# Five feed-forward sections with 13 Strassen groups in place of six with 11, and output chunks added in pairs

## Chip, core and metric

The kernel runs on one core of one Trainium2 chip. The metric is the device time of one execution in microseconds, as the median of several runs; beside it stands one execution under the hardware profiler.

## What is computed

Two residual blocks over 256 tokens of 2048 features, in float32, and a final norm. Each block is a mixer followed by a gated feed-forward part with 5632 hidden features:

```python
def swiglu(h, w_gate, w_up, w_down):
    return (jax.nn.silu(h @ w_gate) * (h @ w_up)) @ w_down

for i in range(DEPTH):            # 2
    h = h + mixer_i(h)            # conv and pooling, then a short conv
    h = h + swiglu(rms_norm(h, ffn_norm[i]), w_gate[i], w_up[i], w_down[i])
return rms_norm(h, final_norm)
```

## The kernel before

Features lie on the 128 partitions and tokens along the rows, so that a chunk is 128 features by 256 tokens; there are 16 chunks of the model width (`NC`) and 44 of the hidden width (`NF`). The residual `h` stays in SBUF throughout.

**A product in three matmuls.** To keep float32 accuracy, every operand is split in a rounded high half and the low rest. `halves_of` (L212) does it for weights: ScalarE copies the high half (L217), VectorE subtracts it to give the low half (L218). `product` (L309) multiplies one block of 128x128 weights with one chunk: high x high, high x low, low x high, three matmuls of 256 columns (L310 to L312), added up in one PSUM bank. A block is one such product.

**Weights** arrive in units of 16 blocks (1 MB) by DMAs from SP's queue (`fetch`, L206) into four buffers, in the order of use. `prepare` (L221) splits them in pieces: 8 blocks for plain units. Five buffers hold the high and five the low halves. `advance` (L250) runs before every block or step and prepares three pieces ahead (`LOOK`).

**The feed-forward part** (`swiglu`, L716) cuts the 44 hidden chunks in sections. `SECTIONS` (L55) lists (groups, direct chunks) of each: `SIZES` are then 9, 6, 8, 7, 7, 7. A *direct* chunk takes 2 x 16 blocks (gate and up, L816 to L840), then on VectorE two scalings by the norm (L476), a product with silu(gate) (L813) and the split into `y` (L336). A *group* makes two chunks at once with a Strassen scheme: in `s_stream` (L781) seven forms instead of eight products, tokens by 256 weight columns, 4 units of 14 steps, each step three matmuls (L794 to L796) into four PSUM banks `s`. A Strassen unit is prepared in four pieces, with the sums of weight blocks that the scheme needs on VectorE (L245 to L248). `combine` (L755) takes the forms together after the group's last unit, seven additions out of PSUM, two `silu` on ScalarE (L775) and two products (L776); `turned` (L745), 20 places later in the order, transposes the result with four TensorE transposes (L750) and splits it into `y` (L752, L753).

**Windows.** The parts of consecutive sections are interleaved. Window w of a feed-forward part holds section w's direct chunks and groups and the down-projection of section w-1: for each of the 16 output chunks one product for each of its hidden chunks, all in one bank out of the pool `acc` (three banks, which the direct chunks and transposes use too), then one addition to `h` (L848) on VectorE. There is one window more than sections, and in the last one the chunk goes on to the next norm (`following.add`, L850): in layer 0 ScalarE and VectorE split it for the second mixer (L338, L339), ScalarE squares it (L447) and GpSimd sums up (L449); in layer 1 ScalarE squares it and multiplies the gain in (L433), and after the 15th chunk it loads the table for the square root (L435). `merged` (L89) writes the order out: runs of 14 Strassen steps spread evenly among the window's plain blocks, after `LEAD` plain blocks (96 in window 0, where the norm and the operands of the Strassen forms are made ready) and before `TAIL` plain blocks (30 in the window of the last section). The two halves of `y` are used in turn by even and odd sections; their sizes follow from the largest section of each kind (`SLOT_A`, `SLOTS`, 9 + 7 slots of 2 KB per partition).

Everything outside `swiglu` is the first mixer (656 blocks), the second mixer (1024 blocks) and the closing norm (L904 to L915).

Of the kernel before, what the change touches and what calls it, by code (L numbers as in the profile page):

```python
# [14 lines left out]
ALU = mybir.AluOpType  # L15
PSUM = bass.MemoryType.PSUM

P = 128
T = 256
D = 2048  # L20
NC = D // P
# [30 lines left out]

SECTIONS = ((1, 7), (2, 2), (2, 4), (2, 3), (2, 3), (2, 3))  # L55
SIZES = [2 * g + p for g, p in SECTIONS]
FIRST = [sum(SIZES[:i]) for i in range(len(SIZES))]
SLOT_A = max(SIZES[0::2])
SLOTS = SLOT_A + max(SIZES[1::2])
LEAD = (96,) + (0,) * len(SECTIONS)  # L60
FORMS_AT, REST_AT = 28, 70
TAIL = (0,) * (len(SECTIONS) - 1) + (30, 0)

# [9 lines left out]
def section_order(i):  # L73

    g, p = SECTIONS[i]
    return list(range(2 * g, 2 * g + p)) + list(range(2 * g))


def window_counts(w):
    blocks = 0  # L80
    if w < len(SECTIONS):
        blocks += SECTIONS[w][1] * 2 * NC
    if w:
# [103 lines left out]
def block_kernel(ctx: ExitStack, tc: tile.TileContext, xT: bass.AP, xtok: bass.AP, vec: bass.AP, wall: bass.AP, out: bass.AP):  # L187
    nc = tc.nc
# [14 lines left out]
    def new_acc(shape=(P, T), name="acc"):  # L203
        return banks["acc"].tile(list(shape), F32, name=name, tag="acc")
# [45 lines left out]
    def advance():  # L250
        t, i = cursor["token"], cursor["piece"]
        while i < len(PIECES) and PIECES[i][0] <= t:
            i += 1
        look = LOOK_M0 if t < M0_BLOCKS else LOOK
        for j in range(cursor["piece"], i + look):
            prepare(j)
        if i + look <= len(PIECES):
            for u in range(PIECES[i + look - 1][1] + 1, PIECES[i + look - 1][1] + AHEAD):
                fetch(u)
        cursor["token"], cursor["piece"] = t + 1, i  # L260

    def next_block():
        assert KINDS[cursor["token"]] == 0
        advance()
        b = cursor["P"]
        cursor["P"] = b + 1
        at = max(k[1] for k in ready if k[0] == "P" and k[1] <= b)
        hi, lo = ready[("P", at)]
        for k in [k for k in ready if k[0] == "P" and k[1] < at]:
            ready.pop(k)  # L270
        o = (b - at) * P
        return hi[:, o : o + P], lo[:, o : o + P]
# [33 lines left out]
                if q:  # L306
                    q.popleft()[1]()

    def product(acc, hi, lo, x, first, last):  # L309
        nc.tensor.matmul(acc, hi, x[:, :T], start=first, stop=False)  # L310
        nc.tensor.matmul(acc, hi, x[:, T:], start=False, stop=False)  # L311
        state_pe["last"] = nc.tensor.matmul(acc, lo, x[:, :T], start=False, stop=last).ins  # L312

    def matmul_chunks(xs, ks, n=1, behind=None, accs=None):


        accs = accs or [new_acc() for _ in range(n)]
        for i, k in enumerate(ks):
            first, last = i == 0, i == len(ks) - 1
            x = xs[k] if isinstance(xs, dict) else xs[:, k, :]  # L320
            for acc in accs:
                hi, lo = next_block()
                product(acc, hi, lo, x, first, last)
                tick()
            if behind is not None:
                behind(k)
        return accs

    phase = [None]
    state_pe = {}  # L330

    def split(dst, src, scale=None):

        if scale is None:
            nc.scalar.copy(dst[:, :T], src)
            nc.vector.tensor_tensor(out=dst[:, T:], in0=src, in1=dst[:, :T], op=ALU.subtract)  # L336
        else:
            nc.scalar.activation(dst[:, :T], src, AF.Copy, scale=scale)  # L338
            nc.vector.scalar_tensor_tensor(out=dst[:, T:], in0=src, scalar=scale, in1=dst[:, :T], op0=ALU.mult, op1=ALU.subtract)  # L339
# [8 lines left out]
    h = act.tile([P, NC, T], F32, name="h")  # L348
    xs_room = act.tile([P, NC * 2 * T + 64], F32R, name="xs")

    def moving(room, at, n):

        return room[:, at // 4 : at // 4 + n * 2 * T].rearrange("p (c t) -> p c t", c=n)
# [119 lines left out]
    def scaled(acc, r, name):  # L473
        pool, tag, bufs = phase[0]
        s = pool.tile([P, T], F32, name=name, tag=tag or name, bufs=bufs)
        nc.vector.tensor_tensor(out=s, in0=acc, in1=r, op=ALU.mult)  # L476
        return s
# [28 lines left out]
    with tc.tile_pool(name="ps0", bufs=5, space=PSUM) as ps0, tc.tile_pool(name="m0", bufs=1) as m0, tc.tile_pool(name="ps_side", bufs=2, space=PSUM) as ps_side:  # L506
# [132 lines left out]
        first = matmul_chunks(xs, every, n=4, behind=loads_behind)  # L639
# [76 lines left out]
    def swiglu(norm, following, at):  # L716
        with tc.tile_pool(name="ffn", bufs=1) as fp:
            phase[0] = fp, "ev", 8
            y = moving(fp.tile([P, SLOTS * 2 * T + 128], F32R, name="y"), at, SLOTS)
# [6 lines left out]
            def rstd():  # L726
                state["rest"] = norm.rstd(keep=rtok, behind=True)

            def token_sums():
                scratch = wst.tile([P, 16 * P], F32, name="w")  # L730
                for k in range(8):
                    later("wait", "form", partial(s_forms, sf, norm, scratch, k))
# [67 lines left out]
            def p_stream(w):  # L800
                if w < len(SECTIONS):
                    g, p = SECTIONS[w]
                    base = SLOT_A * (w % 2)
                    jobs, held = 0, []

                    def gate_of(pair, acc):
                        gate = scaled(acc, state["r"], "gate")
                        nc.scalar.activation(gate, gate, AF.Silu)
                        pair.append(gate)

                    def up_of(pair, c, acc):
                        up = scaled(acc, state["r"], "val")
                        nc.vector.tensor_tensor(out=up, in0=up, in1=pair[0], op=ALU.mult)  # L813
                        split(y[:, base + c, :], up)

                    for c in range(2 * g, 2 * g + p):  # L816
                        pair = []
                        for half in range(2):
                            if w == 0 and jobs in (3, 4):
                                acc = banks["s"].tile([P, 2 * T], F32, name=f"s{jobs - 3}")[:, :T]  # L820
                            else:
                                acc = new_acc()
                            for k in every:
                                yield
                                product(acc, *next_block(), norm.xs[:, k, :], k == 0, k == NC - 1)
                                at = cursor["P"] - first_block
                                if w == 0 and at == FORMS_AT:
                                    token_sums()
                                if w == 0 and at == REST_AT:
                                    state["r"] = state["rest"]()  # L830
                                    while held:
                                        held.pop(0)()
                            jobs += 1
                            if w == 0 and jobs == 1:
                                rstd()
                            evict = partial(up_of, pair, c, acc) if half else partial(gate_of, pair, acc)
                            if "r" in state:
                                evict()
                            else:
                                held.append(evict)  # L840
                if w:
                    base, order = SLOT_A * ((w - 1) % 2), section_order(w - 1)
                    for n in range(NC):
                        acc = new_acc()
                        for i, c in enumerate(order):
                            yield
                            product(acc, *next_block(), y[:, base + c, :], i == 0, i == len(order) - 1)
                        nc.vector.tensor_tensor(out=h[:, n, :], in0=acc, in1=h[:, n, :], op=ALU.add)  # L848
                        if w == len(SECTIONS) and following is not None:
                            following.add(n)  # L850

            for w, kinds in enumerate(WINDOW_KINDS):
                streams = [p_stream(w), s_stream(w) if w < len(SECTIONS) else iter(())]
                for stream in streams:
                    next(stream, None)
                for kind in kinds:
                    next(streams[kind], None)
                    tick()
                    while pending and pending[0][0] <= cursor["token"]:
                        pending.pop(0)[1]()  # L860
                assert all(next(stream, "end") == "end" for stream in streams)
# [40 lines left out]
    last = Norm("final_norm", final=True)  # L902
    swiglu(norm, last, Y_AT)
    halves = rsqrt_of(*last.sums, scale=1.0 / D, halves=True)  # L904
    with tc.tile_pool(name="fin", bufs=1) as fin:

        res = fin.tile([P, 2, NC, P], F32, name="res")
        start = None
        for j, pieces in enumerate((((0, 2), (2, 6), (8, 8)), ((0, 8), (8, 6), (14, 2)))):
            for at, n in pieces:  # L910
                with tc.issue_after(start) if start is not None else nullcontext():
                    part = h[:, at : at + n, j * P : (j + 1) * P]
                    by = halves[j].unsqueeze(1).broadcast_to([P, n, P])
                    start = nc.vector.tensor_tensor(out=res[:, j, at : at + n, :], in0=part, in1=by, op=ALU.mult).ins
# [96 lines left out]
```

## Time and profile before

| | |
|---|---|
| median of 3 runs | 2018.52 us (2014.37, 2018.52, 2018.91) |
| profiled execution | 2013.38 us, its span 2011.3 us |
| TensorE matmuls | 1989.4 us busy, 17386 |
| VectorE | 1692.8 us busy, 2354 instructions |
| ScalarE | 1149.5 us busy, 1511 instructions |
| GpSimd | 206.1 us busy, 184 instructions |
| DMA | 398.27 MB, 198 GB/s in the mean |
| granted TensorE clock | 0.996 in the mean |

The span runs from the first to the last instruction. In the page's slices each digit is the busy share of a fortieth of the span in tenths. A row of a timeline gives start, duration, engine, line, operation and tiles; the idle time before it and what ended it stand in brackets. A row of the groups gives busy time and mean duration, then the engine's idle time just ahead of these instructions.

### The profile page before, as it was taken

To read this page: it belongs to the slowest core of one execution; us is meant where nothing else is said; L and a number is where in the kernel's file an instruction comes from. 1 tells how busy PE (TensorE), PEld (TensorE's weight loads), DVE (VectorE), ACT (ScalarE), POOL (GpSimd) and SP (SyncE) were. 2 spreads that over 40 slices of the span, in tenths; PEclk is the share of its full clock that TensorE was granted. 3 is DMA by queue.
4 is the path that set the end of the run, shared out by engine and by line. 5 is a ranking of instruction groups with operands and counts; after the bars stand their busy time and mean duration, and the time that the engine had idled before them with its cause. 6 is when DMAs were issued, how large, how long until landed. Compare 5 with 4: busy or idle time off the path is not lost.

```text
span 2011.3 us, 41519 instructions
## 1 busy us (share of the span) xinstructions
PE 1989.4 (99%) x17386; PEld 1986.7 (99%) x17386; DVE 1692.8 (84%) x2354; ACT 1149.5 (57%) x1511; POOL 206.1 (10%) x184
## 2 busy tenths in 40 slices
PE   9989999999999999999999999999999999999998
PEld 9989999999999999999999999999999999999997
DVE  6998888898999889998666666788988898899995
ACT  7688675555555555556444444565555555555555
POOL 4996200000000000002000001100000000000003
PEclk9999999999999999999999999999999999999999
DMA  9555445464555555555555555455555555555562
GB/s 361 189 192 208 147 163 204 179 219 187 216 182 225 189 210 202 204 194 219 189 189 192 199 197 189 168 210 189 207 198 204 184 215 192 207 189 194 207 231 82
DMA packets 55772, 398.27 MB, mean 198 GB/s; under 512 B 6304, under 2 KB 6560, under 8 KB 8352
## 3 DMA queue, kind: packets, MB, share of 16 engines
q1 hardware_dynamic: 55584, 395.61, 53.1%
q8 instruction: 136, 2.23, 0.4%
q14 instruction: 52, 0.43, 0.1%
HBM read 393.49 MB, written 2.10 MB: 197 GB/s over the span
## 4 chain that ended last, share of the span: by engine, by line
PE 94%; DVE 4%; ACT 1%; DMA 1%; issue 0%; POOL 0%; DVEq 0%; SPq 0%; ACTq 0%; POOLq 0%
PE acc L312 24%; PE acc L310 24%; PE acc L311 23%; PE s L796 7%; PE s L794 7%; PE s L795 7%; DVE side L537 1%; DVE side L539 1%; DVE lo L218 1%; DMA w<-in_wall 1%; PE acc L750 0%; PE s L312 0%; PE s L310 0%; PE s L311 0%; DVE cat L679 0%
## 5 line engine op out<-in xcount | busy, mean ns | idle before, releaser
L217 ACT CAST hi<-w 128x1024 fp32r<-128x1024 f32 (+1 forms) x917 | 914.9, 1008 | 765.1 <-PE acc L311 460.7
L218 DVE TENSOR_TENSOR lo<-w,hi 128x1024 fp32r<-128x1024 f32 (+1 forms) x865 | 1002.7, 1176 | 200.7 <-ACT hi L217 186.1
L310 PE MATMUL acc<-xs,hi 128*128 128x256 f32 x2544 | 698.9, 276 | 4.7 <-DVE gate L476 2.8
L311 PE MATMUL acc<-xs,hi 128*128 128x256 f32 x2544 | 698.0, 276 | 0.0
L312 PE MATMUL acc<-xs,lo 128*128 128x256 f32 x2544 | 695.8, 276 | 0.1
L310 PEld LDWEIGHTS acc<-xs,hi 128*128 128x128 f32 x2544 | 477.5, 188 | 5.5 <-DVE gate L476 3.0
L311 PEld LDWEIGHTS acc<-xs,hi 128*128 128x128 f32 x2544 | 477.3, 188 | 0.1
L312 PEld LDWEIGHTS acc<-xs,lo 128*128 128x128 f32 x2544 | 475.7, 188 | 0.4 <-DVE lo L218 0.3
L310 PE MATMUL acc<-y,hi 128*128 128x256 f32 x1408 | 388.5, 276 | 0.0
L311 PE MATMUL acc<-y,hi 128*128 128x256 f32 x1408 | 387.6, 276 | 0.0
L312 PE MATMUL acc<-y,lo 128*128 128x256 f32 x1408 | 385.5, 276 | 0.0
L311 PEld LDWEIGHTS acc<-y,hi 128*128 128x128 f32 x1408 | 264.4, 188 | 0.0
L310 PEld LDWEIGHTS acc<-y,hi 128*128 128x128 f32 x1408 | 264.2, 188 | 0.0
L312 PEld LDWEIGHTS acc<-y,lo 128*128 128x128 f32 x1408 | 263.3, 188 | 0.0
L449 POOL TENSOR_TENSOR sumsq<-sumsq,sq 128x256 f32<-128x256 f32 x56 | 54.9, 981 | 1529.4 <-ACT sq L447 1529.2
L794 PE MATMUL s<-hi,sf 128*128 128x256 f32 x704 | 193.7, 276 | 0.0
L795 PE MATMUL s<-hi,sf 128*128 128x256 f32 x704 | 193.3, 276 | 0.0
L796 PE MATMUL s<-lo,sf 128*128 128x256 f32 x704 | 191.7, 276 | 0.0
L795 PE MATMUL s<-hi,xs 128*128 128x256 f32 x528 | 146.1, 277 | 0.0
L796 PE MATMUL s<-lo,xs 128*128 128x256 f32 x528 | 145.9, 276 | 0.0
L794 PE MATMUL s<-hi,xs 128*128 128x256 f32 x528 | 145.7, 276 | 0.0
L794 PEld LDWEIGHTS s<-hi,sf 128*128 128x128 f32 x704 | 132.2, 188 | 0.0
(193 smaller groups left out, 2616.7 us busy)
## 6 DMA issues: line engine op xcount, KB each, us to landing
w<-in_wall SPq DMA_DIRECT2D x365, 1024.0 KB, 4.9
w<-in_wall SPq DMA_DIRECT2D x7, 768.0 KB, 7.8
rows<-in_xtok SPq DMA_DIRECT2D x2, 1024.0 KB, 8.9
h<-in_xT SPq DMA_DIRECT2D x2, 1024.0 KB, 11.8
out<-res SPq DMA_DIRECT2D x2, 512.0 KB, 2.7
w<-in_wall SPq DMA_DIRECT2D x2, 384.0 KB, 3.8
out<-res SPq DMA_DIRECT2D x2, 384.0 KB, 2.7
v<-in_vec SPq DMA_DIRECT2D x1, 260.0 KB, 9.0
```

Source lines behind the costliest of these rows:

```text
L217: state_pe["hi"] = nc.scalar.copy(hi, src).ins
L218: engine.tensor_tensor(out=lo, in0=src, in1=hi, op=ALU.subtract)
L310: nc.tensor.matmul(acc, hi, x[:, :T], start=first, stop=False)
L311: nc.tensor.matmul(acc, hi, x[:, T:], start=False, stop=False)
L312: state_pe["last"] = nc.tensor.matmul(acc, lo, x[:, :T], start=False, stop=last).ins
L449: nc.gpsimd.tensor_tensor(out=self.sums[0], in0=self.sums[0], in1=sq, op=ALU.add)
L537: nc.vector.scalar_tensor_tensor(out=dst, in0=src, scalar=wt, in1=dst, op0=ALU.mult, op1=ALU.add)
L539: nc.vector.tensor_tensor(out=side, in0=side, in1=prods.pop((c, k)), op=ALU.add)
L794: nc.tensor.matmul(acc, xh, hi, start=first, stop=False, skip_group_check=True)
L795: nc.tensor.matmul(acc, xl, hi, start=False, stop=False, skip_group_check=True)
L796: nc.tensor.matmul(acc, xh, lo, start=False, stop=last, skip_group_check=True)
```

## The change

`SECTIONS` becomes five sections of 13, 7, 11, 8 and 5 chunks with 2, 3, 3, 3 and 2 groups and 9, 1, 5, 2 and 1 direct chunks: 13 groups and 18 direct chunks per layer instead of 11 and 22. `SLOT_A` and `SLOTS` follow: 13 + 8 slots of `y`. `LEAD` and `TAIL` are expressions in the number of sections and keep their values at their places. In the down-projection of all windows but the last, two output chunks are accumulated side by side in one bank, only the first matmul of the bank carrying the start flag, and one addition of 128x512 takes both to `h`. The last window goes chunk by chunk as before. The scratch that is set aside in SBUF for dynamic DMA descriptors is set to 1024 bytes.

```diff
-SECTIONS = ((1, 7), (2, 2), (2, 4), (2, 3), (2, 3), (2, 3))
+SECTIONS = ((2, 9), (3, 1), (3, 5), (3, 2), (2, 1))
...
-    def product(acc, hi, lo, x, first, last):
-        nc.tensor.matmul(acc, hi, x[:, :T], start=first, stop=False)
...
+    def product(acc, hi, lo, x, first, last, part=False):
+        nc.tensor.matmul(acc, hi, x[:, :T], start=first, stop=False, skip_group_check=part)
...
-                    for n in range(NC):
-                        acc = new_acc()
-                        for i, c in enumerate(order):
-                            yield
-                            product(acc, *next_block(), y[:, base + c, :], i == 0, i == len(order) - 1)
-                        nc.vector.tensor_tensor(out=h[:, n, :], in0=acc, in1=h[:, n, :], op=ALU.add)
-                        if w == len(SECTIONS) and following is not None:
+                    wide = 1 if w == len(SECTIONS) else 2
+                    for n in range(0, NC, wide):
+                        acc = new_acc((P, wide, T))
+                        for part in range(wide):
+                            for i, c in enumerate(order):
+                                yield
+                                product(acc[:, part, :], *next_block(), y[:, base + c, :], i == part == 0, i == len(order) - 1, True)
+                        nc.vector.tensor_tensor(out=h[:, n : n + wide, :], in0=acc, in1=h[:, n : n + wide, :], op=ALU.add)
+                        if wide == 1:
                             following.add(n)
...
-    nc = _bacc.Bacc("TRN2", target_bir_lowering=False, num_devices=1)
+    nc = _bacc.Bacc("TRN2", target_bir_lowering=False, num_devices=1, dynamic_dma_scratch_size=1024)
```

More of the change, by code (lines that the diff above doesn't have):

```diff
@@ L307, in drain @@
                     q.popleft()[1]()
-    def product(acc, hi, lo, x, first, last):
-        nc.tensor.matmul(acc, hi, x[:, :T], start=first, stop=False)
-        nc.tensor.matmul(acc, hi, x[:, T:], start=False, stop=False)
-        state_pe["last"] = nc.tensor.matmul(acc, lo, x[:, :T], start=False, stop=last).ins
+    def product(acc, hi, lo, x, first, last, part=False):
+        nc.tensor.matmul(acc, hi, x[:, :T], start=first, stop=False, skip_group_check=part)
+        nc.tensor.matmul(acc, hi, x[:, T:], start=False, stop=False, skip_group_check=part)
+        state_pe["last"] = nc.tensor.matmul(acc, lo, x[:, :T], start=False, stop=last, skip_group_check=part).ins
     def matmul_chunks(xs, ks, n=1, behind=None, accs=None):
```

## Prediction

> **What bounds the kernel now.** I read the page first (busy times, slices, chain), then the time of each stage, then the rows of VectorE inside the stages that the change touches.
>
> ```profile
> span 2011.3 us, 41519 instructions
> PE 1989.4 (99%) x17386; PEld 1986.7 (99%) x17386; DVE 1692.8 (84%) x2354; ACT 1149.5 (57%) x1511; POOL 206.1 (10%) x184
> PE   9989999999999999999999999999999999999998
> DVE  6998888898999889998666666788988898899995
> PE 94%; DVE 4%; ACT 1%; DMA 1%; issue 0%; POOL 0%; DVEq 0%; SPq 0%; ACTq 0%; POOLq 0%
> ```
>
> TensorE is busy 99% of the span and owns 94% of the chain, so time goes with its instruction count as long as nothing starves it. But VectorE stands at 8 to 9 tenths throughout both feed-forward parts, and the change puts more on it. Counting blocks in program order (656 in the first mixer, then the windows of layer 0, 1024 in the second mixer) gives the windows' edges. The columns are stretch, length, then PE, PEld, DVE, ACT and POOL busy time, clock, DMA.
>
> ```profile
> 350.30:460.60 110.30, 110.30 (x971) 110.30 (x970) 98.92 (x127) 61.09 (x71) 0.00 (x0) 1.00 0.55 201
> 460.60:576.10 115.50, 115.50 (x1017) 115.50 (x1017) 103.53 (x137) 64.10 (x77) 0.00 (x0) 1.00 0.54 201
> 802.10:902.10 100.00, 100.00 (x880) 100.00 (x879) 93.49 (x122) 58.06 (x68) 0.00 (x0) 1.00 0.53 197
> 802.10:912.70 110.60, 110.60 (x973) 110.60 (x972) 103.36 (x139) 63.15 (x73) 0.00 (x0) 1.00 0.57 211
> 912.70:951.00 38.30, 38.30 (x340) 38.30 (x339) 34.14 (x45) 26.29 (x45) 11.36 (x13) 1.00 0.53 194
> 951.00:1300.50 349.50, 349.50 (x3084) 349.45 (x3083) 238.56 (x315) 154.54 (x179) 16.32 (x31) 1.00 0.54 193
> ```
>
> These are windows 1, 2, 5 (without and with its closing run of 30 plain blocks) and 6 of layer 0, then the second mixer. TensorE has no idle time in any. VectorE's densest stretch, the first 100.00 us of window 5, had it busy 93.49: the nearest thing to what the change asks of it.
>
> **TensorE's share of the change.** A Strassen group is 56 steps where its two chunks done directly are 64 blocks; each is three matmuls. Groups go from 11 to 13 per layer, so 2 x 2 x 8 x 3 = 96 matmuls fall away. The second mixer gives a matmul as 349.50/3084 = 0.1133 us: 10.9 us saved. Each new group adds four transposes. Window 2 holds 336 steps and blocks, 1008 matmuls, 114.2 us at that pace; its other 1.3 us lie on 8 transposes, 0.16 each. Window 1 gives 1.5/8 = 0.19. Sixteen more cost 2.6 at 0.16 (3.0 at 0.19). Net 8.3 us off TensorE.
>
> DMA bytes stay: 4 units of 16 blocks per group against 64 blocks. The loads are issued by SP, none by POOL, so I cost the smaller scratch at nothing:
>
> ```profile
> w<-in_wall SPq DMA_DIRECT2D x365, 1024.0 KB, 4.9
> ```
>
> The denser windows need some 200 GB/s, as window 5's 211 already ran; if the load queue did fall behind, every unit would show as a wait for w.
>
> **VectorE's share.** What an instruction takes of the queue is its distance to the next start, not its duration:
>
> ```profile
> 817.84 1.22 DVE L245 TENSOR_TENSOR w<-w 128x1024 f32<-128x1024 f32 x1
> 818.97 0.69 DVE L753 TENSOR_TENSOR y<-acc,y 128x512 fp32r<-128x512 f32 x1
> 819.57 0.42 DVE L476 TENSOR_TENSOR val<-acc,rstd 128x256 f32<-128x256 f32 x1
> 819.90 0.68 DVE L247 TENSOR_TENSOR w<-w 128x512 f32<-128x512 f32 x1
> 820.50 0.42 DVE L813 TENSOR_TENSOR val<-val,gate 128x256 f32<-128x256 f32 x1
> 820.84 1.22 DVE L218 TENSOR_TENSOR lo<-w,hi 128x1024 fp32r<-128x1024 f32 x1
> ...
> 809.76 0.48 DVE L776 SCALAR_TENSOR_TENSOR v<-v,rtok,c 128x256 f32<-128x256 f32 x1
> 810.15 1.22 DVE L218 TENSOR_TENSOR lo<-w,hi 128x1024 fp32r<-128x1024 f32 x1
> ```
>
> So 1024 columns take 1.13, 512 take 0.60, 256 take 0.335, a product of L776 0.39. A Strassen unit (14 steps, 4.8 us of TensorE) costs 0.60 + 3 x 1.13 for the low halves, 1.13 + 2 x 0.60 for the sums: 6.32. A plain piece of 8 blocks (2.72 us of TensorE) costs 1.13, a group's combination 7 x 0.335 + 2 x 0.39 + 0.60 = 3.73, a direct chunk 4 x 0.335 = 1.34. An addition over two output chunks costs 0.60 (the row of L753, also out of PSUM) where two cost 0.67.
>
> The five new windows ask for: window 1 (240 blocks, 168 steps, 12 transposes, 140.6 us of TensorE) 33.9 + 75.8 + 11.2 + 1.3 + 8 x 0.60 = 127.0, 90%; window 2 136.9, 90%; window 3 128.4, 91%; window 0 behind its opening 96 blocks about the same. Window 4 is the tight one: its last 30 blocks are plain by TAIL, so the 112 steps share the first 242 places with 130 blocks, 82.3 + 1.3 = 83.6 us of TensorE, against 16.25 x 1.13 + 8 x 6.32 + 2 x 3.73 + 1.34 + 6 x 0.60 = 81.4: 97%. The old window 5 by the same prices is 91 in 100.00, where the trace shows 93.49 busy, 2.6% more (a start that waits for a semaphore lies 0.1 later). With that, window 4 is at 100%. Its cover is what VectorE still idles:
>
> ```profile
> L218 DVE TENSOR_TENSOR lo<-w,hi 128x1024 fp32r<-128x1024 f32 x52 | 62.6, 1221 | 4.3 <-ACT hi L217 4.0
> ```
>
> In the old window 5 it mostly waits for ScalarE's high half, which ScalarE (58% busy there) gives as soon as a buffer is free: reserve, which a late VectorE wouldn't wait for. Bounds for window 4: nothing, and 81.4 x 1.026/0.935 - 83.6 = 5.7 us if no more than 93.5% can be had. I take 0.5 per layer, 1.0 in all, near the lower end, since that idle time is reserve.
>
> [...]
>
> **The last window of each layer** has 5 blocks per output chunk instead of 7: 1.70 us where there were 2.38. In layer 0 the next norm's work follows each chunk:
>
> ```profile
> 929.36 0.97 DVE L339 SCALAR_TENSOR_TENSOR xs<-h,v,xs 128x256 fp32r<-128x256 f32 x1
> 930.25 0.41 DVE L848 TENSOR_TENSOR h<-acc,h 128x256 f32<-128x256 f32 x1
> 930.59 1.21 DVE L218 TENSOR_TENSOR lo<-w,hi 128x1024 fp32r<-128x1024 f32 x1
> 931.72 0.97 DVE L339 SCALAR_TENSOR_TENSOR xs<-h,v,xs 128x256 fp32r<-128x256 f32 x1
> ```
>
> That is 0.89 + 0.34 per chunk and 1.13 per 8 blocks; with 5 blocks 1.94 us against 1.70, so VectorE falls 16 x 0.24 = 3.8 us behind. Three accumulator banks forgive two chunks, 3.4. The second mixer then reads the last normed chunk at its 16th block, 5.1 us in; VectorE delivers it near 3.8 + 0.34 + 1.13 + 0.97 = 6.2. I take 1.0, between nothing and 3.8.
>
> In layer 1 the tail pays:
>
> ```profile
> 1995.74 0.42 DVE L848 TENSOR_TENSOR h<-acc,h 128x256 f32<-128x256 f32 x1 [1.96 <-PE acc L312]
> 1998.12 0.42 DVE L848 TENSOR_TENSOR h<-acc,h 128x256 f32<-128x256 f32 x1 [1.96 <-PE acc L312]
> ...
> 1996.53 0.42 ACT L447 ACTIVATE sq<-h 128x256 f32<-128x256 f32 x1 [1.70 <-DVE h L848]
> 1996.98 0.51 ACT L433 ACTIVATE h<-h,v 128x256 f32<-128x256 f32 x1
> 1997.51 1.28 ACT L435 ACT_TABLE_LOAD   x1
> 1998.81 0.20 ACT L435 ACTIVATE warm<-sumsq 128x1 f32<-128x1 f32 x1
> 1998.92 0.40 ACT L447 ACTIVATE sq<-h 128x256 f32<-128x256 f32 x1
> ```
>
> ScalarE's table load after the 15th chunk ends 3.18 us behind that chunk's addition, just as the last square is due. With chunks 1.70 apart, the square is due 0.7 earlier and still waits: +0.7 us.
>
> **Waits.** The wide addition waits for its second chunk, up to 13 blocks (4.4 us) and two Strassen runs later than the first alone. It stands in VectorE's queue behind that chunk's pieces, as the single addition stood; the three banks are needed again only a pair later. No wait for y is moved closer: the last combination of the last section is transposed 20 places after its step, the tail has 30.
>
> **The sum.** -8.3 + 1.0 + 1.0 + 0.7 = -5.6 us on the profiled execution's 2013.38 (span 2011.3 and 2 us around it): 2007.8. The other runs stand at 2014.37, 2018.52 and 2018.91; that scatter is larger than the effect. Against the mean of the four, 2016.3, I forecast 2010.7. About 0.3%, 6.0 us, is what a measurement of this kernel can tell from no change; the forecast lies just inside.
>
> **Rivals.** *VectorE has enough reserve:* both 1.0 terms vanish, only the table load stays, -7.6, 2008.7. For it: window 5 shows 100.00 of 100.00 on TensorE with VectorE at 93.5%. Against it: 97 to 100% leaves nothing.
>
> *VectorE becomes the bound:* it can't pass the 93.5% that the trace ever shows over a window. Window 4 then costs 5.7 per layer, window 3 (93.7% with the 2.6%) 0.3, and the last window of layer 0 its full 3.8: 15.8 in place of 2.0, +8.2, 2024.5: slower. It decides from a ceiling of some 97% down: there window 4 loses 2.5 per layer, which with the 3.8 is more than the 7.6 gained. Against it: in 929.36 to 931.72 VectorE runs without a break.
>
> *The matmuls' pace suffers:* y grows by 5 slots and everything beside it moves in SBUF. Half a percent on the feed-forward parts' 1390 us is 7 us and eats the gain: about 2018, no change. Against it: matmuls over xs, z and y now run at one pace wherever they lie, 0.1133 to 0.114 per instruction in the windows above.
>
> **How the numbers follow.** Forecast 0.65, split by its two unsure terms: under 1.6 together it is beyond 0.3% (0.29), else within (0.36). Enough reserve 0.16, faster. VectorE the bound 0.13: slower 0.11, within 0.02. Pace 0.06: within 0.03, slower 0.03. Together faster 0.45, same 0.41, slower 0.14. The range runs from the lowest execution less the whole 8.3, 2005.1, to 2020.4, half-way from 2016.3 to the slower rival's end; beyond that lies little of that rival's chance.
>
> **What would show it.** 17306 matmuls, 1456 of each Strassen line; 64 additions of 128x512 and 32 of 128x256 in place of 192; VectorE busy up by 4 x (29.0 - 11.7) - 15 = 54 us, to some 1747. Right: idle time on TensorE, if any, stands before L796 or L312 (waiting for a low half) in window 4, and at the second mixer's first chunk. Wrong: such waits in windows 1 to 3, more than 3 us of them in window 4, waits for a bank or for w, or a matmul pace above 0.1135 in the second mixer.

## The result and the profile after

The changed kernel takes 2024.71 us in the median of six runs (2022.43 to 2027.91), the kernel before 2013.85 in six (the three shown ahead and 2013.03, 2013.33, 2012.12). The ratio is 1.0051, with a 95% interval from 1.0039 to 1.0063: slower, by some 10 us, where 5.6 less was forecast. The profiled execution took 2025.58.

These are the span, the busy times and the chain of the page of after:

```profile
span 2023.2 us, 41529 instructions
PE 1992.4 (98%) x17306; PEld 1984.2 (98%) x17306; DVE 1736.6 (86%) x2346; ACT 1163.0 (57%) x1543; POOL 206.4 (10%) x184
PE 88%; DVE 8%; issue 2%; ACT 1%; DMA 1%; SPq 0%; DVEq 0%; POOL 0%; ACTq 0%; POOLq 0%
```

The 17306 matmuls are there as counted: TensorE has 80 fewer. But VectorE's part of the chain has doubled from 4% to 8%, and TensorE's fell from 94% to 88%. The windows, counted as before, are 1, 3, 4 and 5 of layer 0 and the second mixer; columns as before.

```profile
393.80:534.80 141.00, 141.00 (x1238) 141.00 (x1237) 129.58 (x156) 79.15 (x92) 0.00 (x0) 1.00 0.52 197
686.70:829.20 142.50, 142.10 (x1239) 141.55 (x1238) 131.91 (x162) 79.28 (x94) 0.00 (x0) 1.00 0.53 201
829.20:928.20 99.00, 96.70 (x827) 95.29 (x826) 92.08 (x116) 54.76 (x65) 0.00 (x0) 1.00 0.53 203
928.20:957.50 29.30, 28.32 (x244) 27.68 (x244) 26.81 (x42) 20.18 (x38) 11.71 (x12) 1.00 0.59 199
957.50:1307.00 349.50, 349.50 (x3084) 349.45 (x3084) 240.34 (x317) 155.13 (x181) 18.02 (x32) 1.00 0.53 193
```

At 0.340 us per place (three matmuls of 0.1133) and 0.16 per transpose, window 1 should take 408 x 0.340 + 12 x 0.16 = 140.6, window 3 the same, window 4 (272 places, 10 transposes) 94.1 and window 5 (80 and 2) 27.5. Window 1 takes 0.4 more. Window 3 takes 1.8 more, window 4 5.0, window 5 1.8, and only in these three of the windows 1 to 5 does TensorE show idle time. In the kernel before no window behind the opening one is over by more than 0.4. So some 8.6 us per layer are lost where 4.2 were won. In layer 1 the windows come to the same times. The end of the kernel, from the last product on, grows by about 1 us. The rest of the profiled difference, 2.5 us, is not the change's: it lies in the first mixer (250.31 us in this execution, 247.83 in that of before), which is the same in all kernels of this study and takes between 247.0 and 250.5 in their profiled executions.

**What VectorE does in window 4.** Its largest group there, by shape:

```profile
L218 DVE TENSOR_TENSOR lo<-w,hi 128x1024 fp32r<-128x1024 f32 x46 | 54.8, 1219 | 6.5 <-ACT hi L217 6.5
```

It idles 6.5 us ahead of low halves, waiting for ScalarE's high half. The timeline of VectorE in one Strassen unit shows where, and that of ScalarE beside it why:

```profile
889.53 1.21 DVE L245 TENSOR_TENSOR w<-w 128x1024 f32<-128x1024 f32 x1
890.66 0.68 DVE L850 TENSOR_TENSOR h<-acc,h 128x512 f32<-128x512 f32 x1
891.26 0.68 DVE L247 TENSOR_TENSOR w<-w 128x512 f32<-128x512 f32 x1
891.94 1.23 DVE L218 TENSOR_TENSOR lo<-w,hi 128x1024 fp32r<-128x1024 f32 x1
893.08 0.69 DVE L248 TENSOR_TENSOR w<-w 128x512 f32<-128x512 f32 x1
894.96 5.23 DVE L218 TENSOR_TENSOR lo<-w,hi 128x1024 fp32r<-128x1024 f32 x5 [1.20 <-ACT hi L217]
900.11 1.22 DVE L245 TENSOR_TENSOR w<-w 128x1024 f32<-128x1024 f32 x1
```

```profile
890.85 1.05 ACT L217 CAST hi<-w 128x1024 fp32r<-128x1024 f32 x1 [3.26 <-PE s L796]
893.88 4.42 ACT L217 CAST hi<-w 128x1024 fp32r<-128x1024 f32 x5 [1.97 <-DVE w L248]
```

A Strassen unit has four pieces. The third's halves (made of the sum of L245) need only that sum; the fourth's need L247 and L248. Here VectorE's order is sum, sum, low half of the third piece, last sum (L248). ScalarE's next job in its queue is the fourth piece's high half. It starts 893.88, when L248 has ended, though ScalarE had been idle for 1.97 us; the high halves of the plain pieces stand behind it in the same queue. VectorE's next job is the fourth piece's low half, so it stands for ScalarE's 1.05 us and the hand-over: 1.20 us, with nothing between. This is a round trip VectorE, ScalarE, VectorE at a fixed place of each unit. It recurs: three of the window's eight units wait 1.2 us in this way and two 0.84 us with one short instruction (L761) between, 5.3 of the 6.5 us above. One period of this pattern, start of L245 to the next, is 900.11 - 889.53 = 10.58 us; TensorE's share of it is 30.25 places (242 / 8 units), 10.29. Without the 1.20 VectorE would have needed 9.4, so in this unit it is the wait alone that makes VectorE the slower of the two.

The list of all waits has more of these sums for the whole kernel too, first after, then before (total, times, longest):

```profile
ACT hi L217 <- DVE w L245: 187.2, 74, 4.1
ACT hi L217 <- DVE w L248: 149.0, 96, 3.4
```

```profile
ACT hi L217 <- DVE w L248: 118.5, 63, 3.5
ACT hi L217 <- DVE w L245: 55.8, 22, 3.5
```

ScalarE waited for these two sums 85 times before and 170 times after, with 104 units of Strassen weights now and 88 before.

**The fifth window** has another wait. These are TensorE's waits around its start, with the transposes (L750) of the last group:

```profile
928.07 0.41 PE L750 MATMUL acc<-v 128*128 128x128 f32 x2 [1.55 <-DVE v L776]
930.64 0.44 PE L750 MATMUL acc<-v,a 128*128 128x128 f32 x2
931.75 0.50 PE L310 MATMUL acc<-y,hi 128*128 128x256 f32 x2 [0.67 <-ACT y L752]
932.48 0.38 PE L311 MATMUL acc<-y,hi 128*128 128x256 f32 x1 [0.22 <-DVE y L753]
```

The first wait, for the last group's first product, lies at the end of window 4 and is 1.6 of the 2.3 us that TensorE is idle there. The other two are window 5's own: directly behind the second pair of transposes stands the first block that reads their result, and TensorE stands while ScalarE copies the high half of `y` (L752) and VectorE subtracts the low half (L753).

### The profile page after: what moved, and what is told of

Its sections match the earlier page's. It is cut to its first block, busy times and chain, and to the rows that moved or that the text cites. A ratio compares the mean times of both kernels' runs of the same rounds, so it can differ in the third digit from the quotient of the medians.

```text
span 2023.2 us, 41529 instructions
## 1 busy us (share of the span) xinstructions
PE 1992.4 (98%) x17306; PEld 1984.2 (98%) x17306; DVE 1736.6 (86%) x2346; ACT 1163.0 (57%) x1543; POOL 206.4 (10%) x184
## 4 chain that ended last, share of the span: by engine, by line
PE 88%; DVE 8%; issue 2%; ACT 1%; DMA 1%; SPq 0%; DVEq 0%; POOL 0%; ACTq 0%; POOLq 0%
PE acc L311 21%; PE acc L312 21%; PE acc L310 21%; PE s L796 8%; PE s L795 8%; PE s L794 8%; DVE lo L218 3%; DVE side L537 1%; DVE side L539 1%; ACT hi L217 1%; DMA w<-in_wall 1%; PE acc L750 1%; DVE w L245 0%; PE s L310 0%; PE s L312 0%
## 5 line engine op out<-in xcount | busy, mean ns | idle before, releaser
L218 DVE TENSOR_TENSOR lo<-w,hi 128x1024 fp32r<-128x1024 f32 (+1 forms) x897 | 1021.3, 1166 | 165.6 <-ACT hi L217 154.2
L310 PE MATMUL acc<-xs,hi 128*128 128x256 f32 x2288 | 629.1, 277 | 6.3 <-ACT hi L217 3.4
L311 PE MATMUL acc<-xs,hi 128*128 128x256 f32 x2288 | 628.2, 276 | 0.0
L312 PE MATMUL acc<-xs,lo 128*128 128x256 f32 x2288 | 625.0, 276 | 0.1
L310 PEld LDWEIGHTS acc<-xs,hi 128*128 128x128 f32 x2288 | 429.8, 188 | 7.1 <-ACT hi L217 3.8
L311 PEld LDWEIGHTS acc<-xs,hi 128*128 128x128 f32 x2288 | 430.0, 188 | 0.1
L312 PEld LDWEIGHTS acc<-xs,lo 128*128 128x128 f32 x2288 | 427.6, 188 | 0.4 <-DVE lo L218 0.3
L794 PE MATMUL s<-hi,sf 128*128 128x256 f32 x832 | 228.4, 278 | 1.2 <-DVE a L772 0.7
L795 PE MATMUL s<-hi,sf 128*128 128x256 f32 x832 | 226.6, 276 | 0.0
L796 PE MATMUL s<-lo,sf 128*128 128x256 f32 x832 | 221.9, 277 | 0.0
L796 PE MATMUL s<-lo,xs 128*128 128x256 f32 x624 | 172.5, 276 | 0.0
L794 PE MATMUL s<-hi,xs 128*128 128x256 f32 x624 | 172.3, 276 | 0.0
L795 PE MATMUL s<-hi,xs 128*128 128x256 f32 x624 | 172.1, 276 | 0.0
L794 PEld LDWEIGHTS s<-hi,sf 128*128 128x128 f32 x832 | 156.3, 188 | 2.4 <-ACT hi L217 1.2
```

The costliest lines, as they stand in the source:

```text
L218: engine.tensor_tensor(out=lo, in0=src, in1=hi, op=ALU.subtract)
L310: nc.tensor.matmul(acc, hi, x[:, :T], start=first, stop=False, skip_group_check=part)
L311: nc.tensor.matmul(acc, hi, x[:, T:], start=False, stop=False, skip_group_check=part)
L794: nc.tensor.matmul(acc, xh, hi, start=first, stop=False, skip_group_check=True)
L795: nc.tensor.matmul(acc, xl, hi, start=False, stop=False, skip_group_check=True)
L796: nc.tensor.matmul(acc, xh, lo, start=False, stop=last, skip_group_check=True)
```

## Experiments

In kernels with the added order (the first, and those from the fifth on) all lines behind L242 are one higher. Ratios are to the kernel before, run beside each kernel on the same chip. There were three chips (experiments 1 to 4, 5 to 8, 9 and 10), so across these sets ratios compare better than times.

**Sums first.** All of the change, and the third piece's low half is put behind the last sum in VectorE's order; nothing else is changed.

```diff
-        ready[key] = halves_of(w[:, lo : lo + n], S_SHIFT, n, nc.vector)
+        with tc.issue_after(state_pe["sums"]) if what == 2 else nullcontext():
+            ready[key] = halves_of(w[:, lo : lo + n], S_SHIFT, n, nc.vector)
...
-            nc.vector.tensor_tensor(out=w[:, 1536:], in0=w[:, 1024:1536], in1=w[:, 1536:], op=ALU.subtract)
+            state_pe["sums"] = nc.vector.tensor_tensor(out=w[:, 1536:], in0=w[:, 1024:1536], in1=w[:, 1536:], op=ALU.subtract).ins
```

> All work of the changed kernel stays; only the order on VectorE is changed: in every Strassen unit the sums of weight blocks (L247, L248) go ahead of the low half of the third piece. Theory A, the round trip: VectorE is not full in the last sections' window; it idles 0.8 to 1.2 us in each Strassen unit because ScalarE's next high half (and all plain ones queued behind it) waits for L248, which stands behind a low half. Then window 4 of each layer falls from 99.0 to about 95 us, the waits at its end and the start of window 5 shrink, and the kernel comes to 2008 to 2014 us. Theory B, full: VectorE's work alone is too much for TensorE's time; the order changes nothing, 2022 to 2028. Theory C, the pairs in one bank or the moved addresses slow something: 2022 to 2028.

Measured: 2012.03 us, ratio 0.9996 (0.9987 to 1.0005), where the change as it was given has 1.0051. Windows 3, 4 and 5 of layer 0:

```profile
686.30:827.25 140.95, 140.95 (x1238) 140.95 (x1237) 132.80 (x161) 81.76 (x94) 0.00 (x0) 1.00 0.56 203
827.25:921.70 94.45, 94.45 (x829) 94.45 (x827) 91.55 (x115) 53.63 (x64) 0.00 (x0) 1.00 0.55 206
921.70:951.35 29.65, 28.42 (x244) 27.78 (x243) 27.24 (x43) 21.21 (x39) 11.69 (x12) 1.00 0.56 195
```

Window 4 falls from 99.0 to 94.4 and window 3 from 142.5 to 140.95, both without idle time on TensorE, and VectorE does the same work (91.55 us busy, 92.08 before the edit) in 94.45 us: 97% busy. The unit that corresponds to the one above, on VectorE:

```profile
884.79 1.22 DVE L246 TENSOR_TENSOR w<-w 128x1024 f32<-128x1024 f32 x1
885.92 0.69 DVE L851 TENSOR_TENSOR h<-acc,h 128x512 f32<-128x512 f32 x1
886.53 0.68 DVE L248 TENSOR_TENSOR w<-w 128x512 f32<-128x512 f32 x1
887.12 0.68 DVE L754 TENSOR_TENSOR y<-acc,y 128x512 fp32r<-128x512 f32 x1
887.73 0.68 DVE L249 TENSOR_TENSOR w<-w 128x512 f32<-128x512 f32 x1
888.33 6.49 DVE L218 TENSOR_TENSOR lo<-w,hi 128x1024 fp32r<-128x1024 f32 x6
894.74 1.22 DVE L246 TENSOR_TENSOR w<-w 128x1024 f32<-128x1024 f32 x1
```

Six low halves in one run, no wait: the third piece's covers ScalarE's 1.05. The period is 9.95 with one instruction more (L754, 0.60) in it. One order was changed, and the loss of windows 3 and 4 is gone but for 0.4 us each: it was the round trip. That VectorE can't be filled beyond some 93% is refuted.

**Additions one by one.** The new sections with one bank and one addition per output chunk, as before:

```diff
-                    wide = 1 if w == len(SECTIONS) else 2
+                    wide = 1
...
-                        if wide == 1:
+                        if w == len(SECTIONS):
```

> The changed kernel with the old single additions in every window. Theories A and B: VectorE has 0.07 us more for each of 32 pairs per layer, of which the pairs of windows 3 and 4 count: 0 to 3 us slower than the changed kernel, 2024 to 2028. Theory C, the pairs do the harm (a later, longer addition in VectorE's queue): back to 2005 to 2012.

Measured: 2022.98 us, ratio 1.0051 (1.0038 to 1.0064), as the whole change. Windows 4 and 5 of layer 0, and between them a stretch of window 4:

```profile
825.41:927.75 102.34, 98.00 (x831) 97.51 (x829) 92.90 (x125) 53.49 (x64) 0.00 (x0) 0.97 0.55 207
921.90:927.31 5.41, 5.41 (x26) 5.41 (x27) 0.67 (x2) 0.02 (x2) 0.00 (x0) 0.50 0.76 298
927.75:954.95 27.20, 27.20 (x243) 27.20 (x241) 26.15 (x40) 20.80 (x39) 11.71 (x12) 1.00 0.45 155
```

```profile
921.90 0.66 PE L750 MATMUL acc<-v 128*128 128x128 f32 x2 [3.95 <-DVE v L776]
```

All transposes of the last group now stand in window 4, and TensorE waits for its product there, 3.95 us at once. Behind this pause the granted clock is 0.50 for 5.41 us: 26 matmuls take these 5.41 us, where at the pace of the other windows they would take some 2.9. Layer 1 shows the same. So the equal time hides a difference. Some 5 us of this run, an estimate from twice 5.41 less 2.9, are the slower clock, which the changed kernel doesn't have in these windows. Without them windows 3 to 5 would take some 2.4 us less per layer than with pairs, 1.1 of it in window 3 (141.42 for 142.50). The pairs have a share in the loss, then, but they are not what it hangs on: without them VectorE still comes late, and in the first experiment they stay and windows 3 and 4 lose next to nothing.

**Pairs alone.** The old six sections with pairs of output chunks (and the smaller scratch; the diff is against the changed kernel):

```diff
-SECTIONS = ((2, 9), (3, 1), (3, 5), (3, 2), (2, 1))
+SECTIONS = ((1, 7), (2, 2), (2, 4), (2, 3), (2, 3), (2, 3))
```

> The kernel before with the paired additions and the smaller scratch, old sections. Theories A and B: VectorE has reserve there, so as before within 3 us. Theory C: slower than before by 5 us or more.

Measured: 2015.49 us, ratio 1.0012 (1.0003 to 1.0021): slightly slower. Every window but the last agrees within 0.2 us with the kernel before. The last takes 39.95 us where it took 38.34, in layer 1 about as much more, and this is where TensorE waits:

```profile
915.88 0.50 PE L310 MATMUL acc<-y,hi 128*128 128x256 f32 x2 [0.68 <-ACT y L752]
916.60 0.39 PE L311 MATMUL acc<-y,hi 128*128 128x256 f32 x1 [0.23 <-DVE y L753]
```

So the wait for the last group's `y` comes with the pairs (or the scratch, which no run has alone), already in the old sections.

**One group less in the last section** (12 groups per layer; half of the saving is given back):

```diff
-SECTIONS = ((2, 9), (3, 1), (3, 5), (3, 2), (2, 1))
+SECTIONS = ((2, 9), (3, 1), (3, 5), (3, 2), (1, 3))
```

> The changed kernel with 1 group and 3 direct chunks in the last section instead of 2 groups and 1: 12 groups. Theories A and B: window 4 loses its stalls (5 us of its 99.0) and window 5 its 1.8 us wait for y, each per layer, against 2.1 us per layer for the group: 2013 to 2018, as before or little above. Theory C: only the group's 4 us are lost, 2026 to 2032.

Measured: 2013.50 us, ratio 1.0003 (0.9994 to 1.0012). Window 3, unchanged in its work, still takes 142.46; window 4, with 280 places and 4 units instead of 8, takes 96.37, 1.2 over its places alone, about what its transposes need. With half the Strassen units window 4 loses nothing. The round trip would have it so, but less work for VectorE might do the same; this run alone doesn't tell them apart.

**The kernel before with the sums first**, the same edit as in the first experiment:

> The kernel before with the same order on VectorE as the run with the sums first. Theory A, the round trip matters only where VectorE's own cycle with its idle time exceeds TensorE's: TensorE never waited in the old windows, so as before within 2 us, and VectorE's idle time merely moves. A rival, that the order is worth something by itself everywhere (less work on VectorE, other overlaps): 4 us or more faster than before.

Measured: 2012.13 us, ratio 0.9995 (0.9987 to 1.0004), windows within 0.4 us of the unedited kernel's. The old order cost next to nothing there: the same idle time was free as long as TensorE did not run out.

**Sums first, 40 plain blocks behind the last step** instead of 30:

```diff
-TAIL = (0,) * (len(SECTIONS) - 1) + (30, 0)
+TAIL = (0,) * (len(SECTIONS) - 1) + (40, 0)
```

> The run with the sums first, with 40 plain blocks at the end of the last sections' window instead of 30. Its 112 steps then share 232 places with 120 blocks, where VectorE's work is some 100% of TensorE's time. Theory A with VectorE able to run full: the wait for y in window 5 (1.7 us per layer) goes, window 4 loses 0 to 1 us: 2007 to 2011. Rival, the ceiling of 93.5%: window 4 already is above it and slows by 3 us or more per layer, 2015 to 2020.

Measured: 2011.54 us, ratio 0.9991 (0.9982 to 1.0000). Windows 4 and 5:

```profile
824.06:921.83 97.77, 95.85 (x831) 95.04 (x829) 92.54 (x117) 54.46 (x65) 0.00 (x0) 1.00 0.56 205
921.83:949.03 27.20, 27.20 (x243) 27.20 (x241) 26.12 (x40) 20.66 (x38) 11.69 (x12) 1.00 0.54 194
```

Window 5 is down to its 80 x 0.340: no wait for `y` is left in it. But window 4 gets 3.3 us longer, 0.3 of it for the two transposes that moved in. By the prediction's prices VectorE's work beside the first 232 places is 80.0 us (15 plain pieces instead of 16.25), and TensorE's 78.9 + 1.3 = 80.2: all of it. TensorE's waits in this window are 1.2 us for the last group's first product, once, and 0.8 us for high halves; these idle times are not the whole of the 3 us.

**Sums first, 12 groups** (the sums first and one group less in the last section, 30 plain blocks):

> 12 groups (1 group and 3 direct chunks in the last section) with the sums first. Theory A: the 1.5 us of window 3 per layer come back, 2009 to 2012. Theory that window 3's loss has another cause (density alone): as with 12 groups in the old order, 2013 to 2015.

Measured: 2011.28 us, ratio 0.9992 (0.9983 to 1.0000). Windows 4 and 5 of layer 0 take 96.37 and 27.96, against 94.43 and 29.67 with 13 groups. The thirteenth group saves 1.9 us in window 4, and all but 0.2 of it is lost again in window 5, 0.3 for two transposes and most of the rest in the wait for `y`.

**Sums first, and the table loaded early**, behind the 13th instead of the 15th chunk of the last window:

```diff
-                if c == NC - 2:
+                if c == NC - 4:
```

> The run with the sums first, with ScalarE's table load moved from behind the 15th output chunk to behind the 13th of the last window. The forecast's term: the last square is no longer late, 0.7 us off the end of the span, which the profile shows between the last block and the sums' matmul; the times can hardly show it: 2010 to 2013. Rival: the load delays the squares of the 14th and 15th chunk instead and nothing is won.

Measured: 2009.89 us (2007.39 to 2012.25), ratio 0.9979 (0.9970 to 0.9988): faster than both kernels. ScalarE at the end, first of the changed kernel, then of this one:

```profile
2008.87 1.28 ACT L435 ACT_TABLE_LOAD   x1
2010.16 0.20 ACT L435 ACTIVATE warm<-sumsq 128x1 f32<-128x1 f32 x1
2010.27 0.40 ACT L447 ACTIVATE sq<-h 128x256 f32<-128x256 f32 x1
```

```profile
1991.06 1.28 ACT L436 ACT_TABLE_LOAD   x1
...
1993.42 0.42 ACT L448 ACTIVATE sq<-h 128x256 f32<-128x256 f32 x1
...
1995.18 0.42 ACT L448 ACTIVATE sq<-h 128x256 f32<-128x256 f32 x1 [0.80 <-DVE h L851]
```

In the first the last square follows the load without a gap; in the second it waits for its chunk (0.80), no longer for the load. It starts 0.83 us behind the last product's start instead of 1.51, the 0.7 us that were expected.

**The last window's first two chunks interleaved**, on top of that: the blocks that don't read the last group's `y` come first for both.

```diff
+def last_order():
+    size = SIZES[-1]
+    early = size - 2
+    first = [(n, i) for part in (range(early), range(early, size)) for n in range(2) for i in part]
+    return first + [(n, i) for n in range(2, NC) for i in range(size)]
```

> Sums first with the table loaded early, and in the last window the first two output chunks are interleaved: the direct blocks and the first group's blocks of both come first, then the second group's blocks of both, so that the y of the last group is wanted about a chunk later. Theory (that wait is for a late chain of combination, transposes and copy): of the about 1.7 us per layer by which TensorE's fifth window is over its matmuls' own time, about 1.0 goes, 2 us in all: 2006 to 2009 us, against 2009.9 for the same without the interleaving. Rival (the wait comes from the late place of the transposes in TensorE's own order, or from the transposes' bank): nothing won, 2009.5 to 2011. Second rival (the additions of the second chunk come late because both chunks end together, and the second mixer or the tail waits for them): up to 2 us slower, 2011 to 2013.

Measured: 2009.46 us, ratio 0.9984 (0.9976 to 0.9993), and window 5 takes 29.66 as without the edit, with the same waits. The run tells nothing about the theory, because the edit changed nothing that matters: TensorE's matmuls around the window's start come in the same order with and without it. VectorE's first two additions of that window without it show that the scheduler, which sets the order of each engine's queue when the kernel is built, had already interleaved the chunks (a chunk takes 1.70, the additions are 0.58 apart):

```profile
925.20 0.42 DVE L851 TENSOR_TENSOR h<-acc,h 128x256 f32<-128x256 f32 x1 [0.95 <-PE acc L313]
925.78 0.42 DVE L851 TENSOR_TENSOR h<-acc,h 128x256 f32<-128x256 f32 x1 [0.15 <-PE acc L313]
```

**The kernel before with both edits**, sums first and the table early:

> The kernel before with the two edits that helped the changed one, and without the change itself: the low half of a unit's third piece behind the sums, and the table load two chunks earlier. If the gain of the changed kernel with both edits (2009.9, 0.9979) is the new sections' own, this one shows only the earlier table load, at most about 1 us in the tail: 2011 to 2012.5. If the gain is the two edits' alone, it comes to the same 2009 to 2010.5 and the new sections bring nothing.

Measured: 2011.90 us, ratio 0.9996 (0.9987 to 1.0005). With the same two edits the new sections are some 2 us faster: 2009.89, from another chip, or 2009.46 with the ninth experiment's edit, whose interval overlaps this one's a little. The traces agree: from window 0 on a layer's windows take 1.24 us less with the new sections, 2.5 in all, and the end 0.2 more. So that much is theirs; of their 8.3 us on TensorE the rest stays lost, mostly in window 5 (2.1 us over its own time per layer).

## Why the prediction was wrong

**TensorE's saving was right.** 17306 matmuls came out, and in the first experiment windows 3 and 4 need their places and transposes with at most 0.4 us over.

**The step that failed** is "reserve, which a late VectorE wouldn't wait for". From VectorE's idle time ahead of low halves the prediction concluded that it would vanish as VectorE fell behind, because ScalarE is little busy. It didn't: 4.3 us of it in the old window 5 became 6.5 in the new window 4. ScalarE wasn't late for want of a buffer or of time, it was held up by VectorE's own last sum, one instruction earlier. The wait in this ring didn't get shorter with VectorE late, since being late moved both of its ends. The row of the profile had named the releaser, and the prediction didn't ask what released the releaser; the list of waits would have said it, 63 times L248 even then. The term was 0.5 us per layer for window 4 and nothing for window 3; the order alone removed 4.6 and 1.5.

**VectorE's own prices were right.** They asked for 81.4 us of the first 83.6 of window 4, and in the first experiment VectorE is busy for 80.70 of these, without a wait on TensorE; where they ask for all of the time, with 40 plain blocks, TensorE waits. Over the whole kernel VectorE's busy time rose by 44 us where they asked for 54; why it is less was not looked into. Out of PSUM and in SBUF the same 512 columns took the same within 0.02 us: in the first experiment's unit L851, out of PSUM, takes 0.61 to the next start (885.92 to 886.53) and L248, in SBUF, 0.59. The 0.1 of a start that waits shows in the old window 5: L247 starts 1.25 us behind L245, whose result it reads (831.08 to 832.33), and L248 0.72 behind L247, whose result it reads (832.33 to 833.05), each 0.12 over its price.

**The rival that VectorE becomes the bound** gave 2024.5, and 2024.71 was measured, but for another reason. Its ceiling of 93.5% doesn't exist. Its prices were 5.7 for window 4 (4.6 by the edit), 0.3 for window 3 (1.5), and 3.8 at the second mixer's start (nothing). Their sum came near by chance.

**"No wait for y is moved closer"** failed too, a term put at nothing: window 5 is 1.8 us over its own time in the changed kernel and 2.1 with the sums first. In the program the last group is transposed 20 places (6.8 us) behind its last step. On the chip the second pair of transposes starts 12.3 us behind that step's last matmul (918.30 to 930.64), and already 11.2 us in the kernel before. There it cost nothing, since the transposes stand three blocks into the last window, and seven more blocks come before the first matmul that reads their result (the order of the section has five blocks of each output chunk ahead of it, and two chunks are interleaved):

```profile
913.70 0.38 PE L750 MATMUL acc<-v,a 128*128 128x128 f32 x2
916.33 0.39 PE L310 MATMUL acc<-y,hi 128*128 128x256 f32 x2
```

With five chunks in the last section only three blocks of an output chunk, instead of five, don't need the last group's `y`. With two chunks interleaved that is six blocks where there were ten, and the transposes stand behind all six, right ahead of the first reader. TensorE then stands for the copy (0.67 us) and the split (0.22), a round trip with nothing between, as in window 4 but on another engine. That a late product is not needed for this wait shows in the run of the pairs alone, first VectorE, then TensorE:

```profile
911.94 0.48 DVE L776 SCALAR_TENSOR_TENSOR a<-a,rtok,c 128x256 f32<-128x256 f32 x1
914.82 0.38 PE L750 MATMUL acc<-v,a 128*128 128x128 f32 x2
```

The product is ready at 912.42, and the transposes start 2.4 us later without any idle time before them, behind ten blocks: their place in TensorE's order makes the wait there. In the new sections the product is late as well, and the gap ahead of the transposes is some 0.3 to 0.5 us of the 1.8 to 2.1. The tail of 40 blocks moves both, so it doesn't separate them. Why the scheduler puts the transposes so late, with the pairs already in the old sections, stays open.

**The last window of layer 0** was forecast at 1.0 and cost nothing at the mixer: it takes 349.50 us as before. VectorE did fall behind, by less than the 3.8:

```profile
960.36 0.41 DVE L850 TENSOR_TENSOR h<-acc,h 128x256 f32<-128x256 f32 x1
960.70 1.21 DVE L218 TENSOR_TENSOR lo<-w,hi 128x1024 fp32r<-128x1024 f32 x1
961.83 0.47 DVE L339 SCALAR_TENSOR_TENSOR xs<-h,v,xs 128x256 fp32r<-128x256 f32 x1
```

The last addition comes 2.8 us into the mixer and the last normed chunk is ready at 962.30, 4.8 us in, just before its block at 5.1. The lower bound, nothing, was the right one.

**The table load** was forecast at +0.7. The last square starts 1.51 us behind the last product's start, where it was 1.11 in the kernel before, and 0.83 with the load moved forward. So the mechanism was right, but against the kernel before it costs 0.4, because there the square already waited 0.3 for the load. The rest of the 1 us by which the end grew in the profiled execution lies with TensorE's slower clock there, 0.54 from 2012.20 to 2014.40 us: the 16 matmuls of L389 take 2.68 us and the four of L410 1.06, where the kernel before has 2.03 and 0.71 at a clock of 1.00. In the kernels with 12 groups the end is only 0.5 longer, and their mean clock is 0.996, against 0.994 in the changed kernel. With the load moved forward the median falls by more than 0.7, by 2.1 us (2012.03 to 2009.89, on two chips), and no window shows the rest. In the kernel before it brings nothing to speak of (ratios 0.9995 without and 0.9996 with it). **The matmuls' pace** did not suffer: 3084 in 349.50 us in both.

The base was 2.5 us too high: the mean of four executions was 2016.3, the median of six is 2013.85.

## What to carry over

Idle time is reserve only if its releaser does not depend on the idle engine (here 4.3 us of it became 6.5): follow each such wait one step further back, and where it leads back to the same engine, count it as work at its place. When one engine goes from 93% to 97%, look at the order in its queue first, as one instruction moved behind another was worth some 11 us here and next to nothing in the kernel that still had slack. Where a result passes through other engines on its way back, count on the trace, not in the program, how many blocks stand between the step that starts it and its first reader.

## What the runs showed of the hardware

VectorE ran 97% busy over a whole window of 94.45 us, with ScalarE and TensorE beside it, without a wait on TensorE. In the unit of the changed kernel shown above, the hand-over from VectorE to ScalarE took 0.11 us and the one back 0.03: L248's row ends at 893.77, ScalarE starts at 893.88, its first high half ends near 894.93 and VectorE starts at 894.96. The rest of that round trip is ScalarE's own 1.05 us. After a pause of 3.95 us on TensorE, in the run with single additions, the granted clock was 0.50 for the next 5.41 us, and a matmul took some 0.21 us instead of 0.113; after the 1.55 us of the changed kernel it stayed at 1.00.
